# One depthwise filter as matrix products instead of two, and the first pairs' low weights made by accumulating transfers, in a two-layer encoder-decoder block

## The chip, the core and the metric

The kernel runs on one core of a Trainium2 chip. The metric is the device time of one execution in microseconds (us). The engines are TensorE (PE in the rows; PEld is its weight load), VectorE (DVE), ScalarE (ACT), GpSimd (POOL), and SyncE (SP), which here only issues transfers.

## The reference, cut to what matters

Two transformer blocks run one after the other on 1024 tokens of width 1024. The change touches two places: the depthwise convolution of the first block, and the gated feed-forward network, which both blocks have.

```python
def conformer_conv(u, conv_dw, conv_dw_b, conv_ln_g, conv_ln_b, w_conv_pw):
    a, gate = jnp.split(u, 2, axis=-1)
    h = a * jax.nn.sigmoid(gate)
    h = lax.conv_general_dilated(h, conv_dw[:, None, :], window_strides=(1,),
        padding=[(CONV_WIDTH - 1, 0)], feature_group_count=D_CONV) + conv_dw_b   # 31 taps, 512 channels
    h = jax.nn.silu(layer_norm(h, conv_ln_g, conv_ln_b))
    return h @ w_conv_pw

def first_block(x, ...):
    ...
    mixed = jnp.concatenate([attn_out, conv_out], axis=-1) @ w_out
    h = h + rms_norm(mixed, mix_post_g)
    hn = rms_norm(h, ffn_pre_g)
    ff = (jax.nn.silu(hn @ w_gate) * (hn @ w_up)) @ w_down
    return h + rms_norm(ff, ffn_post_g)
```

The second block ends in the same gated network (`w_gu`, `w_down`), with its own norm. All of it is wanted in float32 precision.

## The kernel before

**Precision.** Every large product is made of three TensorE matmuls in a rounded 32-bit format: an operand is split into a rounded part (hi) and what the rounding left (lo), and `mm3` (line 534) issues hi by hi, hi by lo and lo by hi into one sum (lines 539, 540, 541). A hi part is a ScalarE cast. A lo part is made in one of two ways. Either VectorE subtracts hi from the raw tile, or, where `adding` is set, ScalarE writes minus hi from the raw tile (a pass with scale -1 that rounds) and a transfer issued on GpSimd's queue adds the raw tile into it in place.

**Weights.** `Weights.block` (line 125) loads four 128x128 blocks as one transfer of 256 KB on SyncE's queue, and makes hi and lo by either way (lines 141 to 146). The transfers of weights keep their program order (`in_turn`). In the convolution and attention stage `adding` is on; line 1607 turns it off before the first feed-forward network. `Weights.quarter` (line 153) loads a raw row of blocks for the feed-forward network, and `Weights.parted` (line 163) splits such a tile, or a difference of two, by a ScalarE cast (line 168) and a VectorE subtraction (line 169).

**Convolution.** The 31 taps are cut into even and odd taps and even and odd tokens; three filters of 16, 15 and 16 taps on 512 columns, named a, b and c, give the result (`convolve`, line 870, and `join`, line 842). Per channel tile of 128 (i = 0 to 3) VectorE runs each filter as a chain of one multiply per tap (`conv`, lines 835 to 840). For tile i = 3 (`BYPE`) the filters a and b are TensorE products with diagonal weights (`conv_product`, line 850): 16 and 15 blocks, three matmuls each. Filter c of that tile is on VectorE. After `join` come the layer norm (`normed`, line 1005) and the products that read its tiles `ln` (`out1b`, line 1091).

**Gated network.** `gated` (line 1317) multiplies 2x2 blocks by a scheme of seven products, p1 to p7, for each of 22 tiles of the hidden width. Each product is four blocks by three matmuls of 512 columns. The first tiles (`pre`: four in the first network, two in the second) run product by product: p5 and p4 for all of them, then p1, p2, p6, p7, p3, while VectorE is still making the operands of the later products from the normed input. Each tile is a `Pair` (line 1273), whose `ready` calls `parted`. The other tiles run in `tile_steps` (line 1424). Results lie in tiles `ge` and, of the first pairs, in `y` (called early). `put` (line 1325) splits each result for the down product: a cast into a tile `hi`, minus hi into a tile `lo`, an accumulating transfer, and one transfer each to DRAM (`zff`). There are two `hi` and three `lo` tiles.

**Order.** The program's order is not the order on the engines: the tile framework plans each engine's instructions anew, within the number of tiles that `BUFS` (line 40) allows per tag, and places the tiles in the on-chip memory itself, so that a tile of one tag can take over the place of another's. Each engine, and each queue of transfers, then works strictly in its planned order.

Of the kernel before, what the change touches and what calls it, by code (L numbers as in the profile page):

```python
# [10 lines left out]
F32 = mybir.dt.float32  # L11
F32R = mybir.dt.float32r
BF16 = mybir.dt.bfloat16
AF = mybir.ActivationFunctionType
# [24 lines left out]
FOXPER = 1.1  # L39
BUFS = {'phi': 6, 'plo': 6, 'hi': 2, 'lo': 3, 'fs': 2, 'v': 36, 'u': 8, 'p': 4, 'g': 4, 'mm': 7, 's': 3, 't': 3, 'o': 2, 'tmp': 3, 'evt': 3, 'stg': 2, 'rbc': 3, 'turn': 2, 'pt': 2, 'small': 20, 'csmall': 8, 'wraw': 3, 'whi': 8, 'wlo': 8, 'x': 58, 'y': 16, 'ge': 12, 'wt': 5, 'wq': 7, 'r': 16, 'sum': 4, 'rsum': 3, 'f': 6, 'l': 3}  # L40
NPRE = (4, 2)
# [55 lines left out]
class Weights:  # L97
# [64 lines left out]

    def parted(self, raw, eng=None):
        self.made += 1
        w = raw.shape[-1]
        hi = self.pool.tile([P, 512], F32R, tag="phi", name=f"xhi{self.made}", bufs=BUFS["phi"])[:, :w]
        lo = self.pool.tile([P, 512], F32R, tag="plo", name=f"xlo{self.made}", bufs=BUFS["plo"])[:, :w]
        self.nc.scalar.copy(hi, raw)  # L168
        ins = (eng or self.nc.vector).tensor_tensor(lo, raw, hi.bitcast(F32), op=ALU.subtract)  # L169
        self.last_part = ins  # L170
        return hi, lo
# [117 lines left out]
def encoder_decoder_kernel(ctx: ExitStack, tc: tile.TileContext, a: dict, order_out: list):  # L289
# [560 lines left out]
    def conv_product(i, part):  # L850


        src = glu[i][:, hs("ab".index(part))]
        hi, lo = (unit_p("cv", F32R)[:, :16 + HALF] for _ in (0, 1))
        for t in (hi, lo):
            nc.vector.memset(f32(t)[:, :16], 0.0)
        split(hi[:, 16:], lo[:, 16:], src)
        ps = mmps("cv")
        n = 16 if part == "a" else 15
        blocks = [W.block("dw" + part, i, m * P) for m in range(n)]  # L860
        mm3(ps, [(bl, (hi[:, 16 - m:16 - m + HALF], lo[:, 16 - m:16 - m + HALF]))
                 for m, bl in enumerate(blocks)])
        acc = slot("f", HALF)("conv")
        filtered[i, part] = acc
        if part == "a":
            nc.scalar.activation(acc, ps, AF.Identity, bias=pcol("conv_b", i))
        else:
            nc.scalar.copy(acc, ps)

    def convolve(i):  # L870
        for part in "abc":
            if i == BYPE and part != "c":
                conv_product(i, part)
            else:
                conv(i, part)
        join(i)
# [396 lines left out]
    class Pair:  # L1273


        def __init__(self, gate, upm, i):
            self.m = (gate, upm)
            self.i = i
            self.t = {}
            self.parts = {}  # L1280
# [13 lines left out]
        def ready(self, *names):  # L1294
            for n in names:
                if n not in self.parts:
                    self.parts[n] = W.parted(self.get(PRODUCTS[n][0]), nc.vector)
            return self
# [11 lines left out]
    def ahead_pairs(gate, upm):  # L1310

        out = [Pair(gate, upm, i) for i in range(NPRE[gate == "gate2"])]
        for pr in out[:2]:
# [3 lines left out]
    def gated(gate, upm, sums, rb_, a, pre, makers, aside=None):  # L1317
# [73 lines left out]
        for name, e in (("p5", e5), ("p4", e4)):  # L1391
            for i in n:
                ps = product(name, pre[i], sums)
                with tc.high_priority(offset=EVP):
                    nc.scalar.copy(e[i], ps)
        pairs = [Pair(gate, upm, i) for i in n]
        u, g1 = {}, {}
# [209 lines left out]
    W.adding = False  # L1607
    pre = [Pair("gate1", "up1", i) for i in range(NPRE[0])]
    for pr, names in zip(pre, AHEADW):
# [581 lines left out]
def _layout(i):  # L2191
# [9 lines left out]
    c, r = np.arange(512), np.arange(512) % P  # L2201
    for name, first, n in (("dwa", 30, 16), ("dwb", 29, 15)):
        m[name] = np.zeros((512, n * P), np.float32)
        for t in range(n):
            m[name][c, t * P + r] = dw[first - 2 * t]
    wo = f["w_out"]
# [91 lines left out]
```

## Time and profile before

| what | us |
| --- | --- |
| time, median of 3 runs | 2405.27 |
| lowest and highest of the 3 | 2403.38 and 2408.50 |
| the profiled execution, its own time | 2409.36 |
| its span, first to last instruction | 2407.6 |
| TensorE busy in the span | 2355.6 |
| VectorE busy in the span | 1735.1 |

The granted TensorE clock has the mean 0.991 over the span. The profile describes the one profiled execution, so sums are made against 2409.36 us (the span and 1.8 us around it), which is 4.1 us above the median of the three runs. Matmuls overlap, so their durations add up to more than the time they take; the time that one takes in a row of them is read from a window's length over its count.

### The profile page before, as it was taken

How to read it: one execution, taken by the hardware profiler on the slowest of the kernel's cores; microseconds unless marked ns; L12 is line 12 of the kernel's file. 1: busy time of each engine (PE TensorE's matmuls, PEld its weight loads, DVE VectorE, ACT ScalarE, POOL GpSimd, SP SyncE). 2: the span in 40 equal slices, each digit the busy share in tenths (PEclk: the TensorE clock that was granted, in tenths of full speed). 3: DMA queues.
4: the chain of work that ended last, by engine and by line, in shares of the span. 5: the costliest groups of instructions: out<-in, count | busy, mean ns of one | idle time of the engine just before them, and what ended most of it. 6: DMA issues, size and time to landing. Idle time of an engine off the chain costs nothing.

```text
span 2407.6 us, 34907 instructions
## 1 busy us (share of the span) xinstructions
PE 2355.6 (98%) x11985; PEld 1903.0 (79%) x11985; DVE 1735.1 (72%) x3366; ACT 1150.7 (48%) x2333; POOL 271.9 (11%) x351
## 2 busy tenths in 40 slices
PE   9999998998999999999999999998999999999998
PEld 7877787786888887878887778887888888877886
DVE  7987659986767756688545576787787777666667
ACT  6355855555554543244444453545554555442222
POOL 2111220012111100000001110000011111110000
PEclk9999999999999999999999999999999999999999
DMA  7535378369867699724635464123237767699952
GB/s 206 121 82 119 71 181 294 103 172 246 220 177 216 197 368 365 259 73 152 186 118 149 138 208 174 42 57 100 80 106 197 213 173 219 175 270 374 366 177 71
DMA packets 237330, 434.29 MB, mean 180 GB/s; under 512 B 26368, under 2 KB 39008, under 8 KB 237152
## 3 DMA queue, kind: packets, MB, share of 16 engines
q1 hardware_dynamic: 199024, 352.81, 43.3%
q0 software_dynamic: 37840, 79.07, 16.7%
q8 instruction: 94, 1.54, 0.3%
q14 instruction: 84, 0.69, 0.1%
q10 hardware_dynamic: 288, 0.18, 0.0%
HBM read 248.19 MB, written 126.62 MB: 156 GB/s over the span
## 4 chain that ended last, share of the span: by engine, by line
PE 86%; DVE 6%; DMA 4%; issue 2%; ACT 1%; SPq 0%; POOL 0%; DVEq 0%; POOLq 0%; ACTq 0%
PE p L539 10%; PE p L540 10%; PE p L541 10%; PE mm L540 8%; PE mm L539 8%; PE mm L541 8%; PE low L539 6%; PE low L540 6%; PE low L541 6%; PE tp L590 2%; PE lo L1944 1%; DMA wraw<-wstream 1%; PE fo L604 1%; PE swo L951 1%; DMA x<-xT 1%
## 5 line engine op out<-in xcount | busy, mean ns | idle before, releaser
L539 PE MATMUL p<-s,xhi 128*128 128x512 f32 x704 | 276.7, 394 | 0.7 <-ACT xhi L168 0.6
L540 PE MATMUL p<-s,xhi 128*128 128x512 f32 x704 | 277.1, 394 | 0.0
L541 PE MATMUL p<-s,xlo 128*128 128x512 f32 x704 | 271.5, 394 | 2.1 <-DVE xlo L169 2.1
L539 PE MATMUL low<-ff,xhi 128*128 128x512 f32 (+1 forms) x628 | 246.0, 392 | 6.3 <-ACT xhi L168 5.2
L541 PE MATMUL low<-ff,xlo 128*128 128x512 f32 (+1 forms) x628 | 244.0, 392 | 2.7 <-DVE xlo L169 2.7
L540 PE MATMUL low<-ff,xhi 128*128 128x512 f32 (+1 forms) x628 | 245.9, 392 | 0.0
L168 ACT CAST xhi<-wt 128x512 fp32r<-128x512 f32 (+1 forms) x248 | 148.9, 607 | 177.3 <-DVE wt L179 96.2
L539 PE MATMUL p<-x,xhi 128*128 128x512 f32 x528 | 210.1, 398 | 7.4 <-ACT xhi L168 6.4
L540 PE MATMUL p<-x,xhi 128*128 128x512 f32 x528 | 209.1, 396 | 0.0
L541 PE MATMUL p<-x,xlo 128*128 128x512 f32 x528 | 207.1, 396 | 0.0
L169 DVE TENSOR_TENSOR xlo<-wt,xhi 128x512 fp32r<-128x512 f32 (+1 forms) x248 | 166.1, 672 | 51.1 <-ACT xhi L168 37.0
L168 ACT CAST xhi<-wraw 128x512 fp32r<-128x512 f32 (+1 forms) x228 | 134.2, 599 | 106.7 <-PE low L540 58.3
L169 DVE TENSOR_TENSOR xlo<-wraw,xhi 128x512 fp32r<-128x512 f32 (+1 forms) x228 | 150.6, 665 | 41.9 <-DMA lo<-s 14.2
L541 PEld LDWEIGHTS p<-s,xlo 128*128 128x128 f32 x704 | 132.1, 188 | 33.4 <-DVE xlo L169 2.9
L539 PEld LDWEIGHTS p<-s,xhi 128*128 128x128 f32 x704 | 132.4, 188 | 32.3 <-ACT xhi L168 1.6
L540 PEld LDWEIGHTS p<-s,xhi 128*128 128x128 f32 x704 | 132.2, 188 | 30.8
L539 PEld LDWEIGHTS low<-ff,xhi 128*128 128x128 f32 x628 | 118.7, 189 | 34.2 <-ACT xhi L168 6.3
L541 PEld LDWEIGHTS low<-ff,xlo 128*128 128x128 f32 x628 | 118.7, 189 | 30.6 <-DVE xlo L169 3.9
L540 PEld LDWEIGHTS low<-ff,xhi 128*128 128x128 f32 x628 | 118.6, 189 | 26.5
L1332 POOL DMA_DIRECT2D lo<-u x82 | 71.6, 876 | 544.2 <-ACT lo L1331 387.0
L141 ACT CAST whi<-wraw 128x512 fp32r<-128x512 f32 x151 | 91.7, 616 | 83.4 <-DMA wraw<-wstream 43.5
L539 PEld LDWEIGHTS p<-x,xhi 128*128 128x128 f32 x528 | 99.8, 189 | 32.9 <-ACT xhi L168 9.1
(444 smaller groups left out, 5600.6 us busy)
## 6 DMA issues: line engine op xcount, KB each, us to landing
wraw<-wstream SPq DMA_DIRECT2D x416, 256.0 KB, 3.3
ff<-zff SPq DMA_DIRECT2D x308, 256.0 KB, 5.3
zff<-hi SPq DMA_DIRECT2D x154, 256.0 KB, 4.4
zff<-lo SPq DMA_DIRECT2D x154, 256.0 KB, 4.3
lo<-u POOLq DMA_DIRECT2D x82, 256.0 KB, 5.0
lo<-s POOLq DMA_DIRECT2D x66, 256.0 KB, 6.2
wlo<-wraw POOLq DMA_DIRECT2D x64, 256.0 KB, 3.8
res<-zres SPq DMA_DIRECT2D x48, 256.0 KB, 5.7
```

The source lines that it names most:

```text
L141: nc.scalar.copy(hi, raw)
L168: self.nc.scalar.copy(hi, raw)
L169: ins = (eng or self.nc.vector).tensor_tensor(lo, raw, hi.bitcast(F32), op=ALU.subtract)
L539: nc.tensor.matmul(ps, lhsT=ah, rhs=bh, start=first and i == 0, stop=False, skip_group_check=shared)
L540: nc.tensor.matmul(ps, lhsT=ah, rhs=bl, start=False, stop=False, skip_group_check=shared)
L541: nc.tensor.matmul(ps, lhsT=al, rhs=bh, start=False, stop=last and i == n - 1, skip_group_check=shared)
L590: nc.tensor.transpose(ps[:, tsl(j)], pr[:, c0 + (g + j) * P:][:, :P], ident)
L604: nc.tensor.matmul(o[j * 64:j * 64 + 64, :P], lhsT=value(g + t, j), rhs=pts[j][t], start=g + t == 0, stop=g + t == nt - 1)
L951: nc.tensor.matmul(o[j * 64:j * 64 + 64, tsl(bb)], lhsT=vt1[:, kb * P + j * 64:kb * P + j * 64 + 64], rhs=pts[j][:, bb * 256 + 256 - wd[bb ...
L1332: nc.gpsimd.dma_start(lo, t, accum_op=ALU.add)
L1944: nc.tensor.matmul(o[:, tsl(j)], lhsT=lv[t][:, h * P:h * P + P], rhs=pt[t], start=t == 0, stop=t == i)
```

## The change

Filter b of channel tile 3 goes from TensorE to VectorE; the weights `dwb` are no longer loaded. All first pairs, those of `pre` and the second objects `pairs` for the same tiles, take the accumulating way for their low weights. There is a third `hi` and a fourth `lo` tile, and ten `ge` tiles where there were twelve.

```diff
-BUFS = {... 'hi': 2, 'lo': 3, ... 'ge': 12, ...}
+BUFS = {... 'hi': 3, 'lo': 4, ... 'ge': 10, ...}
...
-    def parted(self, raw, eng=None):
+    def parted(self, raw, eng=None, adding=False):
...
         self.nc.scalar.copy(hi, raw)
-        ins = (eng or self.nc.vector).tensor_tensor(lo, raw, hi.bitcast(F32), op=ALU.subtract)
+        if adding:
+            self.nc.scalar.activation(lo, raw, AF.Copy, scale=-1.0)
+            ins = self.nc.gpsimd.dma_start(lo, raw, accum_op=ALU.add)
+        else:
+            ins = (eng or self.nc.vector).tensor_tensor(lo, raw, hi.bitcast(F32), op=ALU.subtract)
...
-        n = 16 if part == "a" else 15
-        blocks = [W.block("dw" + part, i, m * P) for m in range(n)]
+        blocks = [W.block("dwa", i, m * P) for m in range(16)]
...
-        if part == "a":
-            nc.scalar.activation(acc, ps, AF.Identity, bias=pcol("conv_b", i))
-        else:
-            nc.scalar.copy(acc, ps)
+        nc.scalar.activation(acc, ps, AF.Identity, bias=pcol("conv_b", i))
...
-            if i == BYPE and part != "c":
+            if i == BYPE and part == "a":
                 conv_product(i, part)
...
-        def __init__(self, gate, upm, i):
+        def __init__(self, gate, upm, i, adding=False):
...
-                    self.parts[n] = W.parted(self.get(PRODUCTS[n][0]), nc.vector)
+                    self.parts[n] = W.parted(self.get(PRODUCTS[n][0]), nc.vector, self.adding)
...
-        out = [Pair(gate, upm, i) for i in range(NPRE[gate == "gate2"])]
+        out = [Pair(gate, upm, i, True) for i in range(NPRE[gate == "gate2"])]
...
-        pairs = [Pair(gate, upm, i) for i in n]
+        pairs = [Pair(gate, upm, i, True) for i in n]
...
-    pre = [Pair("gate1", "up1", i) for i in range(NPRE[0])]
+    pre = [Pair("gate1", "up1", i, True) for i in range(NPRE[0])]
```

## Rows read from the trace of the kernel before

**Rows 1.** First part of the page: engine, busy us, share of span, instructions.

```profile
PE 2355.6 (98%) x11985; PEld 1903.0 (79%) x11985; DVE 1735.1 (72%) x3366; ACT 1150.7 (48%) x2333; POOL 271.9 (11%) x351
```

**Rows 2.** Windows: length, busy us by engine, granted clock, DMA share, GB/s.

```profile
60.00:120.00 60.00, 60.00 (x274) 48.85 (x273) 58.05 (x100) 17.93 (x33) 7.74 (x9) 1.00 0.52 121
...
660.00:720.00 60.00, 60.00 (x261) 48.63 (x260) 42.01 (x67) 30.73 (x58) 7.49 (x10) 1.00 0.63 172
...
1740.00:1800.00 60.00, 60.00 (x276) 48.58 (x275) 55.05 (x91) 34.02 (x62) 7.95 (x5) 1.00 0.35 95
```

**Rows 3.** The products of filters a and b, by tile `cv`: ns min/median/max, first and last start.

```profile
L541 PE MATMUL cv<-cv,wlo x31: 387/394/504, 190.2 to 215.3; 128*128 128x512 f32 x31
L428 DVE TENSOR_TENSOR cv<-glu,cv x2: 673/676/679, 183.6 to 197.0; 128x512 fp32r<-128x512 f32 x2
```

**Rows 4.** Timeline of VectorE around the filters: start us, us, instruction, count.

```profile
92.84 2.68 DVE L840 SCALAR_TENSOR_TENSOR conv<-glu,const,conv 128x504 f32<-128x504 f32 x4
...
236.66 0.69 DVE L845 TENSOR_TENSOR conv<-conv,conv 128x512 f32<-128x512 f32 x1
...
265.41 2.48 DVE L1027 TENSOR_TENSOR lny<-glu,bc 128x512 f32<-128x512 f32 x4 [2.42 <-PE bc L508]
```

**Rows 5.** Windows between the gated input of tile 3 and the layer norm.

```profile
164.00:236.00 72.00, 72.00 (x410) 56.15 (x409) 57.29 (x147) 37.53 (x102) 12.60 (x17) 1.00 0.49 111
236.00:276.00 40.00, 40.00 (x284) 29.64 (x283) 29.09 (x106) 35.95 (x105) 6.45 (x10) 1.00 0.14 30
```

**Rows 6.** First product that reads the layer norm, by tile `ln`.

```profile
L539 PE MATMUL mm<-ln,whi x32: 387/397/792, 276.2 to 353.3; 128*128 128x512 f32 x32
```

**Rows 7.** Window of the first network's first pairs.

```profile
397.00:514.00 117.00, 109.92 (x508) 86.94 (x507) 117.00 (x195) 61.59 (x113) 6.29 (x4) 1.00 0.42 134
```

**Rows 8.** Timeline of TensorE there: start us, us, instruction, [idle before, releaser].

```profile
410.81 0.50 PE L539 MATMUL p<-s,xhi 128*128 128x512 f32 x1 [0.60 <-ACT xhi L168]
...
417.02 0.50 PE L541 MATMUL p<-s,xlo 128*128 128x512 f32 x1 [2.10 <-DVE xlo L169]
...
457.54 0.32 PE L508 MATMUL bc<-const 128*128 128x128 f32 x1 [1.67 <-POOL const L506]
...
457.95 0.48 PE L541 MATMUL p<-s,xlo 128*128 128x512 f32 x1
...
471.23 0.32 PE L508 MATMUL bc<-const 128*128 128x128 f32 x1 [2.32 <-POOL const L506]
```

**Rows 9.** Timelines of ScalarE, VectorE and GpSimd there.

```profile
454.02 0.62 ACT L168 CAST xhi<-wt 128x512 fp32r<-128x512 f32 x1 [4.83 <-DVE wt L179]
...
456.93 0.67 DVE L169 TENSOR_TENSOR xlo<-wt,xhi 128x512 fp32r<-128x512 f32 x1
...
467.38 3.80 POOL L506 TENSOR_TENSOR const<-const 128x4 f32<-128x4 f32 x1 [9.89 <-DVE const L503]
```

**Rows 10.** Accumulating transfers of results, 500 to 595 us, by tile `lo`; last row: landing.

```profile
L1331 ACT ACTIVATE lo<-u x9: 615/632/656, 518.9 to 577.6; 128x512 fp32r<-128x512 f32 x9
L1332 POOL DMA_DIRECT2D lo<-u x9: 856/860/1212, 519.9 to 578.5; - x9
...
DMA to landing us min/median/max: 2.3/5.0/7.9
```

**Rows 11.** Transfers issued from 60 to 120 us: count, size, median us to landing.

```profile
wlo<-wraw POOLq DMA_DIRECT2D x9, 256.0 KB, 3.4
```

**Rows 12.** The longest wait of TensorE in the gated networks, on TensorE and on ScalarE.

```profile
587.39 0.79 PE L539 MATMUL p<-x,xhi 128*128 128x512 f32 x1 [6.12 <-ACT xhi L168]
...
586.72 0.62 ACT L168 CAST xhi<-wraw 128x512 fp32r<-128x512 f32 x1 [8.00 <-DMA zff<-hi]
```

**Rows 13.** Windows of that stage, and who waited for the transfers to `zff`, 500 to 595 us.

```profile
540.00:600.00 60.00, 52.88 (x214) 41.73 (x213) 40.66 (x65) 33.61 (x62) 13.55 (x16) 0.91 0.91 250
583.00:594.00 11.00, 6.61 (x16) 5.19 (x17) 6.50 (x11) 3.25 (x6) 0.00 (x0) 0.53 0.63 198
  ACT xhi L168: 9.2, 3
```

More of the change, by code (lines that the diff above doesn't have):

```diff
@@ L39 @@
 FOXPER = 1.1
-BUFS = {'phi': 6, 'plo': 6, 'hi': 2, 'lo': 3, 'fs': 2, 'v': 36, 'u': 8, 'p': 4, 'g': 4, 'mm': 7, 's': 3, 't': 3, 'o': 2, 'tmp': 3, 'evt': 3, 'stg': 2, 'rbc': 3, 'turn': 2, 'pt': 2, 'small': 20, 'csmall': 8, 'wraw': 3, 'whi': 8, 'wlo': 8, 'x': 58, 'y': 16, 'ge': 12, 'wt': 5, 'wq': 7, 'r': 16, 'sum': 4, 'rsum': 3, 'f': 6, 'l': 3}
+BUFS = {'phi': 6, 'plo': 6, 'hi': 3, 'lo': 4, 'fs': 2, 'v': 36, 'u': 8, 'p': 4, 'g': 4, 'mm': 7, 's': 3, 't': 3, 'o': 2, 'tmp': 3, 'evt': 3, 'stg': 2, 'rbc': 3, 'turn': 2, 'pt': 2, 'small': 20, 'csmall': 8, 'wraw': 3, 'whi': 8, 'wlo': 8, 'x': 58, 'y': 16, 'ge': 10, 'wt': 5, 'wq': 7, 'r': 16, 'sum': 4, 'rsum': 3, 'f': 6, 'l': 3}
 NPRE = (4, 2)
@@ L1273, in encoder_decoder_kernel @@
     class Pair:
-        def __init__(self, gate, upm, i):
+        def __init__(self, gate, upm, i, adding=False):
             self.m = (gate, upm)
+            self.adding = adding
             self.i = i
@@ L2201, in _layout @@
     c, r = np.arange(512), np.arange(512) % P
[L2202 to L2205, printed above, removed]
+    m["dwa"] = np.zeros((512, 16 * P), np.float32)
+    for t in range(16):
+        m["dwa"][c, t * P + r] = dw[30 - 2 * t]
     wo = f["w_out"]
```

## The prediction

> **What bounds the kernel now.** The first part of the page says TensorE: busy 2355.6 of 2407.6 us, so it is idle for only 52 us in all [rows 1]. What one matmul costs there is not its duration. In a stretch in which TensorE never stops, 261 matmuls fill 60 us, 0.230 us each [rows 2], while a row of them shows 0.394 us [rows 3], because each starts before the one ahead has ended. So an edit can gain in two ways only: fewer matmuls at 0.230 us, or fewer of the 52 us of waits, with the clock that drops after a long one. I read next the windows and, for TensorE's waits and their releasers, the timelines of the three stages that the edits touch: the convolution (164 to 276 us), the first pairs of the first network (397 to 514), and the first tiles after them (540 to 600).
>
> **Filter b leaves TensorE.** It goes from 15 blocks x 3 = 45 matmuls of 512 columns to none: 45 x 0.230 = 10.35 us. TensorE has no gap in the stage [rows 5], so that is time on the path. With it go four loads of 256 KB, their casts and low parts on ScalarE and GpSimd's queue, and a split (0.68 us on VectorE [rows 3]); none of these is late today, I give them nothing. VectorE gains 15 multiplies. Four of them in a row took 2.68 us, so 0.65 to 0.67 us each [rows 4], some 9.9 us, less the split: 9.2 us more. Is there room? From 164 us, when the input of tile 3 is there, to 236, when filter c of that tile ends, VectorE is busy for 57.3 of 72 us [rows 5]. With 9.2 more it is 66.5 of a stretch that shrinks to 61.7. So filter c ends at the earliest at 164 + 66.5 = 230.5, where TensorE's earlier schedule would like 226. What waits for that is the layer norm, and then the products on `ln`, which start at 276.2 [rows 6]. Between the joined filter (236.7) and the norm's last step (265.4) lie 29 us [rows 4], in which ScalarE is the busiest after TensorE (36 of 40 us [rows 5]) with attention work that also moves forward; the norm's own instructions are a small part of it. I take it that most of the lag of 4 to 6 us is absorbed there and 1.4 us is not: **-9 us**. The ends: -10.4, if it is all absorbed, and 0, if the norm does not move at all.
>
> A page and the row differ on the price of a matmul. The Trainium skill ("TensorE: Matmul & The Clock Gate", Back-to-back issue gap) gives a sustained spacing of about 131 ns for 512 columns in a stream with weight loads. By that the edit would be worth 45 x 0.131 = 5.9 us, an estimate; the trace does not agree, at 0.230 us it shows nearly twice that.
>
> **Low weights of the first pairs of the first network.** Four tiles x seven products are 28 low parts. Two are made long before; 26 fall into the stretch from 397 to 514 us, where VectorE is busy for 117.0 of 117 us with 195 instructions, 0.60 us each [rows 7]. The edit takes 26 x 0.60 = 15.6 us from it. ScalarE gets 26 passes of 0.63 us [rows 10], 16 us, and has 55 us free there [rows 7]. GpSimd gets 26 issues of 0.86 us [rows 10], 22 us, where it was busy for 6.3 [rows 7]. In this stretch TensorE idles at the rows shown for 0.60 + 2.10 + 1.67 + 2.32 = 6.7 us [rows 8], all behind VectorE: the casts wait for differences (4.83 us for one [rows 9]), the low part of 417.02 waits in VectorE's queue, and the two norms wait for sums made there. So the edit can return up to 6.7 us.
>
> Against it stands latency. A subtraction takes 0.67 us [rows 9]; the new way is a ScalarE pass of 0.63 and a transfer that lands 5.0 us after its issue in the median, 2.3 to 7.9 [rows 10]. At 417.02 this is about even: the product's first matmul had its rounded part by 410.81, and the subtraction came 6 us later out of VectorE's queue [rows 8]. But for the first p6 the subtraction ended at 457.60 and its matmul began at 457.95 [rows 8, 9]: no room. There the new way ends some 3 us later than today unless the difference, freed of the 14 subtractions ahead of it (two p5, four each of p4, p1 and p2; 14 x 0.60 = 8.4 us), starts as much sooner. GpSimd's queue also carries the power of the norm (up to 3.8 us [rows 9]), for which TensorE waits; it may now stand behind transfers whose ScalarE pass is not done. The ends are -6.7 and +8 us (the latter: the fourth p5, the first p4 and the first p6 each about 2.5 us late). I take **-2 us**, nearer the gain, since VectorE's load is the common cause of all four waits.
>
> **The same in the second network.** Fourteen low parts; where they are used TensorE is busy for 60.0 of 60 us, and VectorE for 55 [rows 2]. There is no wait to win and some room to lose. I take 0, from 0 to +2.
>
> **A rounded and a low tile more, two result tiles fewer.** From 540 to 600 us TensorE is busy for 52.9 us with the transfers at 0.91 of their capacity [rows 13]. The largest wait is 6.12 us at 587.39: the cast of a weight on ScalarE waits 8.0 us for a transfer of a rounded result out of its tile [rows 12], and in this stage casts of weights waited 9.2 us for such transfers [rows 13]. After it the clock is 1.2 GHz instead of 2.4 for a while: mean 0.53 from 583 to 594 us, in which TensorE is busy for 6.6 us [rows 13], half of it lost, 3.1 us. With more tiles ScalarE isn't held so often and the place that a weight takes over was left earlier. That is up to 6.1 + 3.1 = 9.2, and with all the idle time of the stage, 7.1 us, 10.2. The bytes remain, though, and the queues are in order, so that a transfer of a low part on SyncE's queue that waits for its accumulation still holds the weights behind it. I take **-7 us**; the ends are -10.2 and 0. Ten result tiles instead of twelve: four `u`, four `g` and one or two more live at once in the first pairs, which ten just hold; cost 0, at most one transfer's landing, 5 us [rows 10].
>
> **Sum.** -9 - 2 + 0 - 7 = -18 us. The profiled execution of 2409.4 would become 2391.4. It stood 4.1 us above the median, so the predicted median is 2405.3 - 18 = 2387.3 us.
>
> **The rivals.**
> 1. The burst does not shrink. The stage is at 0.91 of the transfers' capacity [rows 13], and more tiles let more of them collide. For: the landing times go to 7.9 us [rows 10]. Against: ScalarE waited for tiles, not for bytes [rows 12]. Then -11 us, 2394.
> 2. VectorE takes the convolution over. If the norm's chain can't start until VectorE is through, TensorE waits for `ln` as long as it saved. For: the lag of 4 to 6 us, and VectorE at 58 of 60 us one stage earlier [rows 2]. Against: 15 us idle from 164 to 236 [rows 5]. Then 0 - 2 - 7 = -9 us, 2396.
> 3. It all cancels: two of the three terms fail at once, or new waits of 10 to 18 us come with the new order of instructions. Within 0.2% of 2405.3.
> 4. Slower: the low weights land late. Ten products of the first pairs (the last two p5, four p4, four p6) follow closely on their weights today. If each low part came 0.63 + 5.0 - 0.67 = 4.9 us later and half of that overlapped, TensorE would wait 10 x 2.5 = 25 us, at a lowered clock for part of it; with -16 from the rest 2414 us. It decides from about 21 us of new waits between 397 and 514 us. Against it: the weights are loaded ahead and six tiles of each kind let several transfers run together.
>
> One rule of the Trainium skill would make rival 4 likelier. From 60 to 120 us, with VectorE busy for 58 of 60 us, nine accumulating transfers of weights landed in 3.4 us in the median [rows 2, 11], less than the 5.0 us of the stage where it is busy for 41 of 60 [rows 10, 13]. The Trainium skill ("SBUF — State Buffer", SBUF: two separate sides) warns that transfers issued from GpSimd starve beside VectorE work that holds the shared port, because their descriptors can't be written. By that rule the 26 transfers beside a saturated VectorE would come late, as in rival 4; so far the trace speaks against it.
>
> **How the numbers follow.** Forecast 0.40; rival 1 0.22; rival 2 0.15; rival 3 0.13; rival 4 0.10. A measurement of this kernel can tell 0.2%, 4.8 us, from no change. Forecast and rivals 1 and 2 are faster by more: 0.77; rival 3 is the same: 0.13; rival 4 slower: 0.10. The best ends together give -10.4 - 6.7 - 10.2 = -27 us, 2378, with some waits beside them that may go too: low end 2375. The high end takes in rivals 1 and 2 and part of 3: 2403.
>
> **What would show it.** In the changed trace: 45 matmuls fewer, and the first product on `ln` at about 267 us instead of 276.2; if it is above 272, rival 2. VectorE below 117 of 117 us in the stretch of the first pairs, which itself is shorter by a few us; waits of TensorE there for a landing of xlo would be rival 4. No wait above 2 us between 540 and 600 us (now earlier by some 11) and no clock below 1.00 there; if it is there still, rival 1. The prediction is wrong outright if new waits of more than 13 us come up elsewhere.

## The result, and the profile after

The changed kernel takes 2428.38 us (median of 2423.17 to 2431.31) where the kernel before, run beside it, takes 2406.89: a ratio of 1.0086 [1.0069, 1.0102]. It is slower by 21.5 us; the prediction said 18 us faster. The profiled execution took 2431.31 us, span 2429.5. The first part of its page, to be read beside [rows 1]:

```profile
PE 2356.8 (97%) x11940; PEld 1906.6 (78%) x11940; DVE 1719.6 (71%) x3336; ACT 1164.8 (48%) x2365; POOL 307.0 (13%) x389
```

The 45 matmuls are gone, yet TensorE is busy for 1.2 us more. Its idle time is 2429.5 - 2356.8 = 72.7 us instead of 52, so 20.7 of the 21.9 us by which the span grew are new waits. The 10.35 us of the matmuls that left are made up by the clock: added up over the records of the granted clock, and leaving out the last 15 us of the span, TensorE ran at 1.2 GHz for 71.7 us, for 34.1 in the kernel before. The waits are in many places. Timeline of TensorE (start, duration, instruction, idle time before it and releaser):

```profile
254.79 0.69 PE L951 MATMUL swo<-pt,vt 128*64 128x128 f32 x2 [4.21 <-ACT pt L943]
...
293.67 0.63 PE L503 MATMUL bc<-constr,sum 128*64 128x1 f32 x16 [3.11 <-ACT cat L970]
...
396.60 0.39 PE L543 MATMUL xk<-memn,whi 128*128 128x256 f32 x1 [3.14 <-ACT whi L141]
...
432.87 0.80 PE L545 MATMUL p<-s,xlo 128*128 128x512 f32 x1 [2.67 <-DMA xlo<-wt]
...
580.37 0.50 PE L543 MATMUL p<-x,xhi 128*128 128x512 f32 x1 [1.50 <-ACT xhi L168]
...
918.24 0.79 PE L543 MATMUL low<-ff,xhi 128*128 128x512 f32 x1 [4.68 <-ACT xhi L168]
...
2241.59 0.79 PE L543 MATMUL low<-ff,xhi 128*128 128x512 f32 x1 [9.82 <-ACT xhi L168]
```

Of [rows 8] the wait of 417.02 has become the one at 432.87, now for a landing; the two norms (457.54, 471.23) wait no more. Of [rows 12] the 6.12 us are 1.50. The rest is new or longer. How late TensorE is at the same work tells where the time went. Each number is its start there less that in the kernel before (first column); the next four columns are kernels with a part of the change, told below.

| TensorE reaches | before, us | changed | filter | low weights | tiles | low weights + tiles |
| --- | --- | --- | --- | --- | --- | --- |
| first product on `ln` | 276.2 | +5.6 | +4.3 | -0.2 | -0.4 | +0.5 |
| first matmul of gated network 1 | 393.2 | +12.0 | +5.3 | +4.8 | -0.3 | +4.4 |
| 48th | 420.8 | +18.7 | +5.5 | +12.9 | +1.1 | +12.0 |
| 240th | 475.1 | +12.0 | +7.0 | +5.8 | +0.5 | +4.8 |
| 600th | 559.9 | +18.5 | +8.0 | +11.0 | +1.7 | +9.7 |
| 1000th | 663.3 | +9.2 | +1.4 | +3.3 | -6.5 | +2.4 |
| 200th of the down products | 909.6 | +12.7 | +1.0 | +3.4 | -4.6 | +6.4 |
| query product, block 2 (`nq`) | 1407.6 | +11.7 | +0.2 | +2.1 | -4.1 | +6.0 |
| first product on `xn` | 1590.4 | +16.6 | -0.2 | +3.5 | -4.5 | +13.1 |
| 961st of the down products | 2176.3 | +13.3 | +2.2 | +1.7 | -8.6 | +9.1 |
| 1301st | 2265.7 | +21.4 | -0.1 | -0.8 | -2.2 | +15.2 |
| end of the span | 2407.6 | +22.0 | +0.4 | -1.2 | -2.0 | +15.4 |

A single execution lies up to some 4 us off its median, so steps in a column are read here and the price of a kernel from its median.

### The profile page after: what moved, and what is told of

It is laid out like the page before. It is cut to its first block, busy times and chain, and to the rows that moved or that the text cites. A ratio compares the mean times of both kernels' runs of the same rounds, so it can differ in the third digit from the quotient of the medians.

```text
span 2429.5 us, 34925 instructions
## 1 busy us (share of the span) xinstructions
PE 2356.8 (97%) x11940; PEld 1906.6 (78%) x11940; DVE 1719.6 (71%) x3336; ACT 1164.8 (48%) x2365; POOL 307.0 (13%) x389
## 4 chain that ended last, share of the span: by engine, by line
PE 85%; DMA 5%; DVE 4%; ACT 3%; issue 3%; SPq 0%; POOL 0%; DVEq 0%; ACTq 0%; POOLq 0%
PE p L545 11%; PE p L543 11%; PE p L544 11%; PE mm L544 7%; PE mm L543 7%; PE mm L545 7%; PE low L543 6%; PE low L545 6%; PE low L544 6%; PE tp L594 2%; PE lo L1945 1%; DMA wraw<-wstream 1%; DMA zl<-stg 1%; PE fo L608 1%; DMA x<-xT 1%
## 5 line engine op out<-in xcount | busy, mean ns | idle before, releaser
L173 DVE TENSOR_TENSOR xlo<-wt,xhi 128x512 fp32r<-128x512 f32 (+1 forms) x224 | 149.8, 671 | 68.0 <-ACT xhi L168 41.9
L173 DVE TENSOR_TENSOR xlo<-wraw,xhi 128x512 fp32r<-128x512 f32 (+1 forms) x210 | 138.7, 663 | 22.8 <-ACT xhi L168 7.0
L543 PEld LDWEIGHTS low<-ff,xhi 128*128 128x128 f32 x628 | 119.1, 190 | 43.4 <-ACT xhi L168 16.6
```

The source lines that it names most:

```text
L543: nc.tensor.matmul(ps, lhsT=ah, rhs=bh, start=first and i == 0, stop=False, skip_group_check=shared)
```

## The parts one by one

| kernel | median, us | ratio to before, 95% |
| --- | --- | --- |
| filter alone | 2409.42 | 1.0016 [1.0001, 1.0031] |
| all low weights alone | 2409.59 | 1.0016 [1.0006, 1.0025] |
| tiles alone | 2409.66 | 1.0017 [1.0005, 1.0029] |
| low weights and tiles | 2425.15 | 1.0083 [1.0066, 1.0101] |

They ran beside a kernel before of 2407.06.

```diff
-            if i == BYPE and part != "c":        # filter alone
+            if i == BYPE and part == "a":
...
-        out = [Pair(gate, upm, i) ...            # low weights alone, in all three places
+        out = [Pair(gate, upm, i, True) ...
...
-'hi': 2, 'lo': 3, ... 'ge': 12                   # tiles alone
+'hi': 3, 'lo': 4, ... 'ge': 10
```

> Only filter b of channel tile 3 goes to VectorE; pairs and tiles as before. Theory A (VectorE has no room for the filter when it is needed, so the layer norm and the attention work beside it are late): the first gated product starts about 12 us later than before (405 instead of 393), and nothing later gives that back: 2419 us. Rival B (the filter itself gains its 10 us; the loss comes from the transfers and the tiles of the gated networks): 2397 us, the first gated product at about 383.

> Only the low weights of the first pairs by accumulating transfers; filter b on TensorE and the tiles as before. Theory A: the waits that it adds (low weights that land late, 3 us) and the waits for the norms' powers that it takes away (4 us) cancel: 2404 to 2410 us. Rival B (the pairs' transfers are late and push everything): 2416 us or more.

> Only a third hi and a fourth lo tile, and ten ge tiles. Theory A: the wait of 6.1 us at 587 with its slower clock goes (9 us), and the two waits before the down products (4.7 at 918 and 9.8 at 2241 in the changed kernel, 2.1 and 3.1 before, with their clock some 12 us) come with these tiles: 2410 us. Rival B (the tiles do what they are for, and the later waits come from elsewhere): 2397 us.

> The changed kernel with filter b back on TensorE. Theory A (the filter is the larger part of the loss): 2416 us, and the first gated product starts at about 393 us. Rival B (the filter is a gain of 10 us that the rest hides): 2438 us.

For the filter alone neither theory's number came: the median lies between them, 10 us from one and 12 from the other. Low weights alone and tiles alone came within the numbers of their theories A; low weights and tiles together lie between their two theories again, 9 and 13 us away. By the medians each part costs about 2.5 us alone, 7.5 in sum; the intervals of the ratios reach from nearly nothing to 7 us for each. Low weights and tiles together cost 18.1, and the filter adds 3 to that. So the loss is no single part's, and the parts do not add.

The table of TensorE's starts shows where they do not. In its last row the three parts alone add to -2.8 us, and the changed kernel stands at +22.0. Of these 24.8 us 13.2 lie between the 600th and the 1000th matmul of the gated network, where the kernel before has its wait of 6.12 us [rows 12]. There each part alone gains on it (filter 6.6, low weights 7.7, tiles 8.2 us: 22.5 in sum), and the changed kernel gains 9.3. The prediction put what that wait and its clock can give at 9.2 us: it can be won once, and the sum of the parts counts it three times. Another 4.3 us lie between the query product and `xn`, and 6.5 between the 961st and the 1301st of the down products. The next three sections take each part; the fourth takes what else happens when they meet.

## The filter: what TensorE wins is lost at the norm

The windows (length, busy us by engine, clock, DMA share, GB/s) first of the changed kernel, then of before around the join of [rows 4]:

```profile
164.00:207.00 43.00, 43.00 (x251) 33.25 (x250) 35.79 (x87) 21.09 (x61) 7.21 (x10) 1.00 0.44 104
207.00:254.00 47.00, 43.00 (x295) 32.54 (x293) 44.02 (x153) 32.11 (x108) 5.31 (x9) 1.00 0.19 46
254.00:276.00 22.00, 20.45 (x127) 15.10 (x128) 11.34 (x22) 11.17 (x24) 3.35 (x4) 0.84 0.00 1
```

```profile
207.00:236.00 29.00, 29.00 (x155) 23.00 (x154) 22.07 (x59) 15.92 (x41) 6.69 (x8) 1.00 0.58 127
236.00:256.00 20.00, 20.00 (x155) 13.77 (x153) 17.81 (x72) 17.71 (x61) 0.80 (x2) 1.00 0.01 2
```

And VectorE's timeline in the changed kernel, at the start of filter b and at the join:

```profile
207.31 0.48 DVE L839 TENSOR_SCALAR conv<-glu,const 128x512 f32<-128x512 f32 x1
...
254.37 0.77 DVE L849 TENSOR_TENSOR conv<-conv,conv 128x512 f32<-128x512 f32 x1
```

Filter b begins at 207, when tile 2 is through, and from there both filters of tile 3 go tap by tap between steps of the attention's softmax. The join is at 254.4 instead of 236.7: 17.7 us later, not the 4 to 6 that I worked out from idle time. VectorE is busy for 44.0 of these 47 us. The attention work that it did after the join before (17.8 of 20 us from 236 to 256) is now done ahead of it, and TensorE's share of that attention too; after the join nothing is left to do but the norm (VectorE 11.3 and ScalarE 11.2 of 22 us), and TensorE waits (at 254.79 still for an attention tile, and at 293.67).

Two runs split this.

```diff
-"b": ([dw[i][:, 29 - 2 * m:30 - 2 * m] for m in range(15)], None),
+"b": ([dw[i][:, 29 - 2 * m:30 - 2 * m] for m in range(1 if i == BYPE else 15)], None),   # the filter alone otherwise
```

> The kernel before with filter b of channel tile 3 taken off TensorE and put on VectorE with its first tap only: the 14 multiplies of the other taps are left out, so this part of the convolution is not computed. It splits the filter's edit in two: TensorE loses the 45 matmuls, VectorE gains next to nothing. Theory A (what ate the 10.35 us is VectorE's longer chain: with both chains the join came 18 us later): without the multiplies the join is at or before 236.7 us, the first product on ln at about 266, and the median is 2397. Theory B (the 45 matmuls were work that TensorE did while ScalarE and VectorE were busy with attention anyway; without them it waits for that): waits of TensorE of 3 us and more on ScalarE's attention tiles between 236 and 300 us stay as they are with the whole filter, and the median is 2403 to 2408.

Measured: 2397.43, ratio 0.996 [0.9945, 0.9975], 9.9 us below before. The median is theory A's, but it was not reached in theory A's way. The first product on `ln` starts at 271.1 us, where theory A said 266 and the kernel before has 276.2; the join is at 239.5, not at or before 236.7. The first matmul of the gated network is 3.5 us earlier than before, the 600th 4.5, and the 1000th 11.2: 6.7 us of the gain come with the wait of 6.12 us at 587 again (here the largest from 540 to 600 us is 1.53), a wait that the low weights and the tiles each take away as well. Of theory B's waits on attention tiles (the 4.21 us) nothing is left, but TensorE waits for the norm all the same, and the clock drops behind it. Timeline of TensorE, then the window from there, in this run:

```profile
285.30 0.92 PE L499 MATMUL bc<-constr,sum 128*64 128x1 f32 x14 [4.82 <-DVE sum L456]
```

```profile
285.00:300.00 15.00, 14.70 (x69) 12.03 (x70) 5.63 (x11) 7.74 (x14) 3.24 (x4) 0.82 0.47 98
```

So the 45 matmuls are worth their time only as long as TensorE has other work. The 79 matmuls that start between 246 and 256 us in the kernel before start 9.7 us earlier here in the median (7.8 to 12.1), near 45 x 0.230 = 10.35. Then 4.82 us go in the wait and, at a mean clock of 0.82, 0.18 x 15 = 2.7 us behind it. Those 9.7 us also settle the price in favour of the row: the Trainium skill ("TensorE: Matmul & The Clock Gate", Back-to-back issue gap) gives 131 ns, by which it would have been 5.9 us, an estimate. The 14 multiplies cost 2409.42 - 2397.43 = 12 us between the two runs, 9.4 of them at the first product on `ln`, as much as their own 9.3.

```diff
-'f': 6                                           # the filter alone otherwise
+'f': 8
```

> The kernel before with filter b on VectorE, as in the run with the filter alone (2409.4), and eight tiles for filters where there were six. Theory A (filter b began only at 207 us because its tile came free late, and from there the two chains of tile 3 took turns): b begins before 190 us, the join is at about 242 instead of 254, the products on ln begin at 270 or earlier, and the median is 2400. Rival (the order of the chains is the plan's, whatever tiles there are): b begins at 206 to 208 again and the median is 2409.

Measured: 2414.58, 1.0034 [1.0021, 1.0047]. Filter b began at 211.6 and the join came at 255.6: the rival holds, the order of the chains is the plan's. That it is 5 us worse than with six tiles comes from somewhere else, told below.

## The low weights: the late ones gain, the early ones lose

```diff
-        out = [Pair(gate, upm, i, True) ...      # late only: p5, p4 keep the subtraction
+        out = [Pair(gate, upm, i) ...
```

> The kernel before with accumulating low weights only in the second objects of the first pairs (products p1, p2, p6, p7, p3: 20 low parts in the first network, 10 in the second); p5 and p4 keep VectorE's subtraction. Theory A (with all of them the loss is the landing of the first p5 low weights, 3 us at 427, and the gain the norm's two waits at 457 and 471, which were 4 us): no wait for a landing before 440 us, the two waits of the norm gone, and the median is 2402. Rival (the waits on casts of weights at 379 to 387 us, before any of these transfers, come with the plan, which is made anew for any such edit): they are there in this kernel too, 4 to 6 us in all, and the median is 2408 to 2411.

Measured: 2400.51, 0.9975 [0.9965, 0.9985]: 6.8 us faster than before, and the best kernel here that computes all. Window of its first pairs, beside [rows 7], and the two norms of [rows 8]:

```profile
397.00:514.00 117.00, 113.77 (x524) 89.94 (x523) 104.31 (x172) 69.94 (x130) 24.14 (x24) 1.00 0.69 180
```

```profile
451.83 0.60 PE L512 MATMUL bc<-const 128*128 128x128 f32 x4
...
466.68 0.60 PE L512 MATMUL bc<-const 128*128 128x128 f32 x4
```

VectorE has 12.7 us to spare and the norms' waits (1.67 and 2.32 us) are gone. This is the gain that the prediction worked out, and in its place it is there: TensorE is 5.4 us ahead of before at the 240th matmul. But at the 600th it is 0.7 us behind, and the 5.9 us by which it leads at the 1000th come with the wait of 6.12 us, of which 2.44 are left here. That the norms' gain reaches the end is not shown.

```diff
-    pre = [Pair("gate1", "up1", i) ...           # early only, network 1: p5, p4
+    pre = [Pair("gate1", "up1", i, True) ...
```

> The kernel before with accumulating low weights only for p5 and p4 of the first network (eight low parts); the later products keep the subtraction. Theory A (the two halves add: all of them +2.5, the late ones -6.8): +9, so 2416, with waits on casts and low parts of weights from 379 to 387 us of 5 to 7 us in all, a wait of 3 us for a landing at about 427, and the two waits of the norm (1.7 and 2.3 us) as before. Rival (the halves don't add; the early ones are harmless alone): within 3 of before, 2404 to 2410.

Measured: 2413.67, 1.003 [1.0018, 1.0041], 7.3 us slower than before (2406.35): theory A. The halves nearly add, -6.8 and +7.3 against +2.5 for all of them (four early ones of the second network are in neither). Two things make the loss. The waits of TensorE before and at the first products, with all low weights:

```profile
378.96 0.39 PE L543 MATMUL xk<-memn,whi 128*128 128x256 f32 x1 [1.58 <-ACT whi L141]
382.14 0.58 PE L543 MATMUL xk<-memn,whi 128*128 128x256 f32 x1 [2.68 <-ACT whi L141]
387.20 0.58 PE L543 MATMUL xk<-memn,whi 128*128 128x256 f32 x1 [1.94 <-ACT whi L141]
...
427.46 0.79 PE L545 MATMUL p<-s,xlo 128*128 128x512 f32 x1 [2.98 <-DMA xlo<-wt]
```

The first three come behind the two low parts that are made long before their product, which the prediction gave nothing. With all low weights they are transfers too, issued on GpSimd's queue 15 to 20 us earlier:

```profile
359.57 0.86 POOL L171 DMA_DIRECT2D xlo<-wt  x1 [5.18 <-ACT xlo L170]
...
364.40 0.86 POOL L171 DMA_DIRECT2D xlo<-wt  x1 [2.94 <-ACT xlo L170]
```

The windows of that stretch, before and with all low weights:

```profile
356.00:374.00 18.00, 18.00 (x81) 14.76 (x80) 16.76 (x29) 6.87 (x12) 0.86 (x1) 1.00 1.06 361
```

```profile
356.00:374.00 18.00, 18.00 (x81) 14.76 (x80) 13.25 (x24) 7.39 (x13) 2.62 (x4) 1.00 1.05 323
```

The transfers are at their limit in both, at 1.06 and 1.05, but with the two more among them they move 323 GB/s instead of 361, and SyncE's queue falls 3 us behind in an order of tiles that is the same up to 376 us. SyncE in the kernel before, then with all low weights:

```profile
369.56 0.33 SPq L115 DMA_DIRECT2D wraw<-wstream  x1
370.18 1.01 SPq L704 DMA_DIRECT2D x<-xT  x2
371.60 0.99 SPq L115 DMA_DIRECT2D wraw<-wstream  x2
```

```profile
372.66 0.33 SPq L115 DMA_DIRECT2D wraw<-wstream  x1
373.30 1.04 SPq L708 DMA_DIRECT2D x<-xT  x2
374.68 1.67 SPq L115 DMA_DIRECT2D wraw<-wstream  x2
```

Weights that are read 3 us later are cast 3 us later. All four kernels that have these two transfers, and filter b on TensorE, need 14 to 15 us from the first read of `x` to this weight; the ten without the two need 11 to 13. The fourth wait is for the low part of the third p5, and here the transfers themselves were late: five issued from 418 to 430 us, and the windows of that stretch, before and with all low weights:

```profile
DMA to landing us min/median/max: 6.6/8.5/9.5
```

```profile
418.00:430.00 12.00, 12.00 (x52) 9.48 (x52) 12.00 (x20) 7.59 (x15) 0.00 (x0) 1.00 0.48 171
```

```profile
418.00:430.00 12.00, 6.93 (x16) 4.47 (x17) 10.40 (x18) 8.57 (x16) 4.36 (x5) 0.67 1.06 348
```

They landed after 8.5 us, not 5.0 [rows 10], in a stretch where the transfers are at 1.06 of their capacity, twice the share of before. The Trainium skill ("SBUF — State Buffer", SBUF: two separate sides) would blame VectorE's hold on the shared port. The rows speak more for the load of transfers: VectorE is busier (58 of 60 us) where such transfers landed in 3.4 us at a share of 0.52 [rows 2, 11]. No run changed one without the other.

```diff
-        pairs = [Pair(gate, upm, i, True) ...    # late only, network 1
+        pairs = [Pair(gate, upm, i, gate == "gate1") ...
```

> The kernel with late accumulating low weights (2400.5), in the first network only; the second network's first pairs keep the subtraction. Theory A (the gain is the first network's: the norm's two waits and VectorE's load from 440 to 514 us): 2400 to 2402. Rival (part of it is the second network's, where TensorE waited 2.7 us for a low part on VectorE at 2168 us, which is gone with the late ones in both): that wait is back, and the median is 2403 to 2405.

Measured: 2402.60, 0.998 [0.9971, 0.999]: the first network's late ones alone give a gain too. What the second's add, 2 to 3 us by the medians, cannot be told from nothing, as the two intervals overlap; the prediction put zero. The wait for a low part is back (2.44 us at 2163), but it stands in the kernel with all low weights as well (2.44 at 2168.51), so it does not hang on the second network's subtraction.

## The tiles: the gain comes where forecast and is given back

With the tiles alone the largest wait from 540 to 600 us is 1.71 us instead of 6.12, and TensorE is 6.5 us ahead at the 1000th matmul (forecast: 7). Window beside [rows 13], then a wait later on:

```profile
540.00:600.00 60.00, 57.33 (x244) 45.09 (x243) 43.51 (x71) 36.68 (x68) 14.65 (x17) 1.00 0.97 273
```

```profile
2219.55 0.79 PE L539 MATMUL low<-ff,xhi 128*128 128x512 f32 x1 [8.19 <-ACT xhi L168]
```

At the second down product TensorE stands for a weight: 8.19 us, 3.14 in the kernel before (at 2221.34). Every transfer there is at the limit (share 1.05 from 2160 to 2225 us), and SyncE's queue is in order. Reads of operands that stand between the last weight before that wait and the next one, in the kernel before, with the tiles alone, and in the changed kernel:

```profile
ff<-zff SPq DMA_DIRECT2D x36, 256.0 KB, 5.7
```

```profile
ff<-zff SPq DMA_DIRECT2D x45, 256.0 KB, 5.3
```

```profile
ff<-zff SPq DMA_DIRECT2D x46, 256.0 KB, 5.4
```

With more tiles for results the plan puts ten more reads of 256 KB ahead of that weight. They leave this queue about 0.65 us apart, some 6 us; the two weights are 39.3 us apart instead of 30.0, and the wait is 5 us longer. (One more lies outside of that window; in the planned order it is 36 in each kernel with the tiles of before and 46 in each with all the new ones.) And the gain in the first network is not the tiles' own: with the filter alone the wait of 6.12 us is 1.41, with all low weights 1.85, with the late ones 2.44. Each of these edits took most of it, and where it was gone the tiles had little left to win; why edits so different all take it is not shown.

```diff
-'ge': 10
+'ge': 12                                         # the changed kernel otherwise
```

> The changed kernel with twelve result tiles again instead of ten; all else as changed. Theory A (ten just hold; the loss is elsewhere): 2428, within 3. Rival (the two missing tiles hold up the first pairs or the first tiles after them, which is why low weights and tiles together cost 18 us and each alone 2.5): the waits of TensorE between 500 and 600 us shrink below 2 us, and the median is 2412 to 2418. A third case: a few instructions only change places and the time moves by over 3 us without any wait between 397 and 600 us being another; then the late waits (at 918, 1434 to 1456, 1676 and 2241 us) hang on the plan's order and not on tiles.

Measured: 2430.27, 1.0097 [1.0082, 1.0112]: theory A, the two result tiles fewer cost nothing that can be told.

## When the parts meet: order and places

> The kernel with accumulating low weights for p1, p2, p6, p7 and p3 only (2400.5) and the changed numbers of tiles (three hi, four lo, ten result tiles). Theory A (that low weights and tiles together cost 18 us and each alone 2.5 comes with the early low weights, those of p5 and p4): the tiles add what they add alone, so 2403, and no wait above 6 us at the start of either down product. Rival (any accumulating low weights together with more tiles do it, because the plan of the whole rest is made anew): waits of 5 to 10 us at about 905 and 2230 us and new ones between 1415 and 1460, and 2412 to 2418.

> As the run with early accumulating low weights alone (p5 and p4 of the first network), with the changed numbers of tiles. Theory A (the early low weights and the tiles are what costs 18 us together): 2424 or more, with waits of 4 us and more at about 912 and of 8 us and more at about 2236. If the costs only add: what the early ones give alone and 2.5 more. Rival (the late ones and the tiles are the pair): the same as the early ones alone, within 3.

Measured: late low weights with tiles 2414.72, 1.0028 [1.0018, 1.0039]; early ones with tiles 2422.57, 1.0065 [1.005, 1.008]. So the tiles add 2.6 us to the kernel before, 14.2 to the late, 8.9 to the early and 15.6 to all low weights. My theory that the early ones are the partner fell; the rival holds. A part of it is the wait of 6.12 us, which the late low weights and the tiles each win alone, and together only once. In that pair, between the query product and `xn` of the second block, TensorE falls 5.5 us behind, although each engine has exactly the same sequence of instructions there as in the kernel before. What differs is who waits: ScalarE's casts into the staging tiles `stg` wait for the transfer out of the same place. None of them waits so in the kernel before, with the filter, the tiles or the late low weights alone; they wait for some 22 us in all in the changed kernel, with eight filter tiles, and with late low weights and tiles (21.7, 22.5 and 22.2). Two staging tiles is the number in `BUFS`, yet in the kernel before more are in flight: the cast at 1411.95 below begins while the transfers of the tile two ahead land until 1415.5. So this kind of tile has more places there than its number, and where they are lost its casts queue behind transfers. To see this without any part of the change:

```diff
-'u': 8, 'p': 4, 'g': 4                           # the kernel before otherwise
+'u': 9, 'p': 4, 'g': 4                           # one run; the other: 'u': 8 and 'g': 5
```

> The kernel before with nine tiles instead of eight of the kind u, which no part of the change touches; in this build all four casts of the keys into staging tiles wait for transfers, where before it was one. Theory W: waits of TensorE of 1.2 to 1.8 us at about 1411, 1426 and 1443 us, the second gated network begins 5 to 6 us later than before, and the median is 2411 to 2413. Rival (those waits are made up for later, or need more tiles or low weights beside them): within 2 of before, 2405 to 2409.

> The kernel before with five tiles instead of four of the kind g. The order is that of before on TensorE and ScalarE, and three instructions move on VectorE and on SyncE's queue; only the places of tiles, and with them 148 of ScalarE's waits, are others. The casts of the keys wait as before. Theory W says that places matter where a transfer's landing is waited for, which is not so here: within 2 of before, 2405 to 2409. Rival (any new set of places moves the time by 5 us or more): outside that.

Measured: with nine `u` 2417.44, 1.0049 [1.0034, 1.0064]; with five `g` 2408.59, 1.0007 [0.9993, 1.0021]. ScalarE in the kernel before, then with nine `u`, then TensorE there:

```profile
1406.53 0.59 ACT L427 CAST stg<-kn 128x512 fp32r<-128x512 f32 x1
1411.95 1.08 ACT L427 CAST stg<-kn 128x512 fp32r<-128x512 f32 x2
1417.39 0.59 ACT L427 CAST stg<-kn 128x512 fp32r<-128x512 f32 x1
```

```profile
1411.48 0.59 ACT L427 CAST stg<-kn 128x512 fp32r<-128x512 f32 x1 [6.27 <-DMA zl<-stg]
1416.14 0.59 ACT L427 CAST stg<-kn 128x512 fp32r<-128x512 f32 x1 [3.91 <-DMA zl<-stg]
1417.79 0.59 ACT L427 CAST stg<-kn 128x512 fp32r<-128x512 f32 x1 [1.05 <-DMA zl<-stg]
1421.81 0.59 ACT L427 CAST stg<-kn 128x512 fp32r<-128x512 f32 x1 [2.75 <-DMA zl<-stg]
```

```profile
1412.84 0.50 PE L539 MATMUL mm<-nq,whi 128*128 128x512 f32 x1 [2.45 <-DVE stg L428]
...
1428.08 0.43 PE L604 MATMUL co<-pt,vc 128*64 128x128 f32 x2 [1.12 <-ACT pt L421]
```

A tile more of a kind that the change never touches costs 12.7 us; in its trace TensorE falls 8.8 us back between the query product and `xn`, more than the 5 to 6 expected. Its order is not quite that of before (some 150 of 11985 matmuls moved), so the late low weights with tiles, whose order in this stretch is the same, are the cleaner case for the places. The same stretch costs 4.9 us in the changed kernel and 5.5 with eight filter tiles, about what that run was worse. Other places alone (five `g`) change nothing that can be told.

```diff
-'hi': 3, 'lo': 4, 'ge': 10                       # late low weights otherwise
+'hi': 2, 'lo': 4, 'ge': 12                       # one run; the other: 'hi': 3, 'lo': 3, 'ge': 12
```

> Late low weights (2400.5) and one more lo tile only: two hi, four lo, twelve result tiles. In SyncE's order the weights of the second down product then stand behind 35 reads of operands since the last weight, as without more tiles (36), and not behind 46; but the staging tiles have no more than two places. If both causes hold: the wait at about 2215 is 5 us or less, the waits at 1411 to 1443 are there (4 to 5 us in all), and the median is 2405 to 2407. Rival for X (more tiles delay those weights whatever the order): a wait of 8 us at 2220 and 2411 or more. Rival for W: no waits at 1411 to 1443 and 2400.

> Late low weights (2400.5) and one more hi tile only: three hi, three lo, twelve result tiles. Here 35 reads of operands stand ahead of the second down product's weights, but 40 instead of 32 ahead of the first one's, and the staging tiles have places enough. If both causes hold: no waits at 1411 to 1443, a wait of 5 us or less at 2215, and one of 6 to 9 us instead of 3.9 at about 903; the median is 2402 to 2405. Rival (tiles cost whatever the order): 2411 or more.

Measured: a `lo` tile more 2415.91, 1.004 [1.0024, 1.0055]; a `hi` tile more 2402.86, 0.9985 [0.9974, 0.9996]. The `hi` tile is as both causes say: no staging waits, 2.70 us at 2218, and 4.22 at 906, less than I gave it. The `lo` tile has the staging waits as expected, but 6.78 us at 2228 too, with only 35 reads ahead of that weight, and 2411 or more was the rival's number. The count of reads is a part of that wait, not the whole.

> Filter b on VectorE and late low weights, with the numbers of tiles of before. Alone they gave +2.4 and -6.8 us. If costs add: 2403. Theory W says more: in this kernel too the staging tiles have only two places, though no number of tiles was changed, so 5 to 6 us come on top: 2407 to 2409, with waits of TensorE of 1.2 to 1.8 us at about 1411, 1426 and 1443.

Measured: 2413.10, 1.0026 [1.0017, 1.0035], 10 us above what the two parts add to, with the staging waits (18.9 us on ScalarE) and 4.9 us lost between the query product and `xn`. So it needs no more tiles. The rest of that surplus is of the size of the wait won twice: from the 600th to the 1000th matmul the filter alone gains 6.6 us on before, the late low weights alone 6.6, and the two together 6.1.

```diff
-'stg': 2                                         # late low weights and tiles otherwise
+'stg': 4
```

> The run with late low weights and the changed numbers of tiles (2414.7), with four staging tiles in the second block's attention instead of two. Theory W (5 to 6 us of its loss are ScalarE's casts into staging tiles, at 1409 to 1434 us, that wait for the transfer out of the same place): the waits of TensorE at about 1411, 1426 and 1443 us (1.3, 1.2 and 1.8) go, and the median is 2409, within 2. Rival (they are the shadow of something earlier, as norms or weights that come late): the waits stay or move, and the median is 2413 to 2416. The wait at 2227 us (8.3) stays in both cases.

Measured: 2413.65, 1.0025 [1.0016, 1.0034], no better than without by more than the noise. The waits for staging tiles are gone, but the order moved on every engine (on VectorE some 290 of 3336 instructions), and TensorE now waits 1.86 us for a sum and 3.75 us for the transfers `lqk` in the same stretch. The rival's number holds: removing those waits did not return their price. Whether the next thing in that chain was as late anyway or the new order made it so is not shown, and so the price of the staging waits by themselves is not either.

## Why the prediction was wrong, point by point

- **What bounds the kernel.** Right: what was won or lost is in TensorE's waits and the clock after them, and 0.230 us a matmul holds as long as TensorE has work (9.7 of 10.35 us). Wrong is the step from there, "TensorE has no gap in the stage, so that is time on the path": with hardly a multiply in its place 3.5 us of it were left at the gated network. That this run's median shows 9.9 us is luck, the wait at 587 us.
- **Filter, -9.** Wrong by 11 us; +2.4 alone, and without the gain at 587 us, which is not its own, more: +5.3 at the gated network, +8.0 at the 600th matmul. Beside the path, the step that failed is the lag: I divided VectorE's idle time, as if the chain could fill it, and took the remaining 29 us as a place that absorbs. The chain goes tap by tap behind attention work, 1.5 us a tap (31 taps in 47 us), and that attention work was the cover which the norm's chain needed. Rival 2 named this mechanism and put the mark at 272 us; the first product came at 281.8.
- **Low weights of the first network, -2, and of the second, 0.** Together +2.5, inside the ends. The right rows were read, but as one term it hid two of opposite sign: late -6.8, early +7.3. The late ones' own gain, 5.4 us at the 240th matmul, is gone by the 600th. Rival 4's mechanism, late landing, is real at one product out of the ten and gone after; its price there was a wait of 3 us. The term that the prediction put at nothing without a reason is the two low parts "made long before": as transfers they hold up weights by 3 us, and the first gated matmul is 4.8 us late (low weights alone).
- **Tiles, -7.** The size was right in its place (6.5 us) and the stage right too. The step that failed is that it would last and be the tiles' own: later stages, the second down product above all, took most of it back, and the parts beside it had already taken the same wait.
- **The sum.** The step that cost most is the addition itself. Costs alone add to +7.5 us; together they are +21.5. Each term was priced as if it alone met the kernel before; but the wait of 6.12 us can be won once, and filter, low weights and tiles each win it alone (22.5 us in sum, 9.3 together). The rest is new waits at staging tiles and at the down products. The prediction's last sentence named it (new waits of over 13 us elsewhere) and rival 3 had "new waits of 10 to 18 us" at 0.13, set against gains which were not there or were one gain counted three times. Slower had 0.10, for a mechanism that turned out small.

Still open: whether the norms' gain of the late low weights reaches the end, what each of the late waits in the changed kernel would be worth alone, since no run took one away without moving others, and why a `lo` tile more holds up the second down product.

## What to carry to other kernels

Where a planner makes order and places anew, price an edit also by what it does to stages that it doesn't touch: run it alone, with its neighbours, and beside an edit that means nothing there. A gain from a single long wait belongs to whoever comes first; don't add two edits that win the same wait, and look in the trace whether an edit's gain arose in its own stage before you credit the edit. Split an edit by when its pieces are used, as the late low weights alone gave 6.8 us that the early ones hid.

## What was not expected of the hardware

The same kind of accumulating transfer of 256 KB landed in 3.4 us at a transfer share of 0.52, in 5.0 at 0.91 and in 8.5 at 1.06, beside a VectorE busy for 58 of 60, 41 of 60 and 10 of 12 us. In these windows the landing goes with the load of transfers and not with VectorE's busy time; no run varied one alone.
